# A hybrid encoder layer on one Trainium2 core: the second token group's projections, nine pairs of them as block products in a stage of their own, and attention as one stream over all heads

## The chip, the cores and the metric

The kernel runs on one core of one Trainium2 chip. TensorE (PE) multiplies matrices out of SBUF into PSUM, VectorE (DVE), ScalarE (ACT) and GpSimd (POOL) work element by element, and SyncE (SP) issues most of the transfers between DRAM and SBUF. The metric is the device time of one execution in microseconds; less is better.

## What the reference computes

One layer over 1280 tokens (a prompt of 1024 and a sample of 256), with 2048 channels, in fp32:

```
h    = rmsnorm(x, norm_w)
proj = h @ w_in                    # 2048 -> 4*1024 + 5*1024 + 16 columns
na_q, na_k, na_v, na_g, ml_qk, ml_v, ml_o, ml_z, ml_gp = split(proj)
att  = neighbourhood_attention(na_q, na_k, na_v, rpb) * silu(na_g)      # 8 heads of 128, 8 x 16 window
qk   = silu(centred_depthwise_conv(ml_qk, width 5))                     # 2048 channels
h    = bidirectional_mlstm(*split(qk), ml_v, gates(ml_gp))              # 4 heads of 256
mem  = rmsnorm(h) * sigmoid(ml_o) * silu(ml_z)
y    = rmsnorm(x + concat(att, mem) @ w_out, final_norm_w)
```

Prompt and sample go through the same weights; attention, convolution and mLSTM don't cross from one to the other.

## The kernel before, in words

Each fp32 operand of a large matmul is split into a high part (a cast by ACT, L156) and a low part (the difference, by DVE, L157), and each product takes three matmuls: high by high, high by low, low by high. So a product over 128 input channels is three passes, and a projection over 2048 channels is 48.

The tokens are worked on in two groups. Group A is tokens 0 to 767, group B the last 256 of the prompt and the 256 of the sample, 512 in all. Output channels come in blocks of 128, numbered: 0 to 7 are Q of the attention heads (`QT0`), 8 to 15 K (`KT0`), 16 to 23 the gate G (`GT0`), 24 to 39 the convolved channels of the mLSTM (`QK0`; 24 to 31 its Q, 32 to 39 its K), 40 to 47 O (`OT0`), 48 to 55 Z (`ZT0`). Two neighbouring blocks form a *pair*, named by its first number. V is projected in eight *units* V0 to V7 (`proj_v`), V4 with the 16 mLSTM gate columns beside it.

The program has three parts.

1. *Group A.* Each pair is computed in `pair_a` by seven block products in place of eight: tokens, input channels and output channels are halved, and sums of blocks are multiplied. For a pair's weights, POOL forms four sums of blocks in `summed` (L499), named by their product's number: 5, 6, 7 and 3. They live in SBUF only.
2. *Group B.* `proj_pair` computes a pair as 96 matmuls of 128x512 (L641): four loads of 512 KB of weights (`w_piece`, L618), eight splits of 512 columns, and a scaling by the inverse norm (L242). Q and K are stored split, convolved channels go through the convolution (L398, L404, L410), the rest is stored as it is to the scratch `pT` in DRAM. `proj_v` has 192 matmuls of 256 columns (272 in V4; L728). Group B's input is split when it is first used (`LazyX`, L149).
   Attention runs among these projections. After the projections of two attention heads and one mLSTM head, `run` emits their units at high priority: neighbourhood attention (`na_sample`, `na_prompt`) and mLSTM (`ml_units`). Blocks G, O and Z of group B come last, in `late_gate`: attention has by then stored its result without that factor for the tokens of group B, and `late_gate` reads it back from the scratch `mixT` (`lt`, L693), multiplies and stores it again (L695).
3. *W_out.* `product` (L1462, 128x512) multiplies the mixed channels, again by seven block products. `mix_block` loads the 32 blocks of `mixT` (L1342), `y_init` the residual (L1419), both issued by SP.

The order on each engine comes from the scheduler of the tile framework, which simulates the program and takes instructions by priority, and from the buffers of each pool: PSUM has three banks tagged "pr" and five tagged "a"; `po` is a ring of 520-column buffers; the pool "att" holds attention's buffers and is opened before the first pair of group B.

Of the kernel before, what the change touches and what calls it, by code (L numbers as in the profile page):

```python
# [35 lines left out]
XFIRST = (0, 1, 8, 9, 2, 3, 10, 11, 4, 5)  # L36
QT0, KT0, GT0, QK0, OT0, ZT0 = 0, 8, 16, 24, 40, 48


@with_exitstack  # L40
def kernel(
# [41 lines left out]
    qb = [dram.tile([P, 4], F32, tag=f"qb{n}", name=f"qb{n}") for n in range(16)]  # L83

    ident = const.tile([P, P], F32, tag="ident", name="ident")
    make_identity(nc, ident)
# [368 lines left out]
    def pair_a(n1, bg=iter(()), hook=None):  # L455
# [31 lines left out]
        for r in range(4):  # L487
# [122 lines left out]
    def po(name):  # L610
        return wb.tile([P, 520], F32, tag="po", name=name, bufs=NPO)
# [9 lines left out]
    def w_split(raw, lo_, hi_, name):  # L621
# [3 lines left out]
        return t  # L625

    FORTH = ((0, 1), (0, 0), (1, 0))

    def proj_pair(n1, X, late=False):
# [16 lines left out]
        for j in range(2):  # L646
            o = po(f"pco{n1}_{j}")
            if QK0 <= n1 < OT0:
# [8 lines left out]
                )  # L657
                cv = po(f"pcv{n1}_{j}")
                for _ in conv_taps(cv, o, ct, 516, 0):
                    pass  # L660
                hi = wb.tile([P, 520], F32R, tag="po", name=f"pch{ct}", bufs=NPO)
                store_conv(ct, cv, hi, o, ((0, 258, GA - 2), (260, 516, TP)))
                continue
# [12 lines left out]

    def late_gate(n1, k0, X):
        os_ = None
        if k0 >= 8:
            os_ = proj_pair(n1, X, True)  # L680
            for o_ in os_:
                S.activation(o_, o_, AF.Tanh, scale=0.5)
            n1 += ZT0 - OT0
        for j, z_ in enumerate(proj_pair(n1, X, True)):
            k = k0 + j
# [3 lines left out]
            sc = 0.5  # L689
            if k >= 8:  # L690
                V.scalar_tensor_tensor(z_, os_[j], 1.0, z_, op0=ALU.add, op1=ALU.mult)
                sc = w4_sb[:, k - 8 : k - 7]
            DM.dma_start(th, mixT[k][:, GA:])  # L693
            V.scalar_tensor_tensor(z_, th, sc, z_, op0=ALU.mult, op1=ALU.mult)
            DM.dma_start(mixT[k][:, GA:], z_)  # L695

    def proj_v(u, X):
# [38 lines left out]
        for tt in range(nt):  # L736
# [3 lines left out]
            if gates:  # L740
# [3 lines left out]
                )  # L744

    att_ctx = ExitStack()
    ap = att_ctx.enter_context(tc.tile_pool(name="att", bufs=2))

# [37 lines left out]
    def na_sample(h):  # L786
# [35 lines left out]
        o = na_tile("nst", [P, NAK], f"{nm}ot", 3)[:, :TS]  # L822
        S.copy(o, b[:, :TS])
        DM.dma_start(mixT[h][:, TP:], o)
        yield

    def na_prompt(h):
# [3 lines left out]
        def setup():  # L831
# [4 lines left out]
            o = na_tile("not", [P, TP], f"{nm}o", 1)  # L836
            DM.dma_start(o[:, :GA], pT[GT0 + h][:, :GA])
            hd["q"], hd["k"], hd["o"] = q, k, o
            yield

        def block(c4):
# [48 lines left out]
            for o, m in ends:  # L890
# [8 lines left out]
            cs = slice(c4 * 16, c4 * 16 + 16)  # L899
            ng = GA // 64  # L900
            V.scalar_tensor_tensor(
                ov[:, :ng, cs], bv[:, :ng], 0.5, ov[:, :ng, cs], op0=ALU.mult, op1=ALU.mult
            )
            S.copy(ov[:, ng:, cs], bv[:, ng:])
            if c4 == 3:
# [7 lines left out]
    def ml_tris():  # L913
        t = mid("tris")
        return [
# [4 lines left out]
    def ml_gates(sq, tris):  # L920
# [6 lines left out]
        def sm(name):  # L927
            return ap.tile([P, nt, 8], F32, tag=f"{nm}{name}", name=f"{nm}{name}", bufs=1)

        bd, bo, em = (sm(n) for n in ("bd", "bo", "em"))  # L930
        tmp = mid(f"{nm}tmp")
        lf, e, PL, EX, tot, mc, a1, mF = (
# [22 lines left out]
        rows = []  # L955
        rfi, rma = ([f(hf(f"{nm}r{w_}{i}"))[0:8, :TP] for i in range(2)] for w_ in "im")
        for r_, (w_, src) in enumerate((("f", lf), ("i", ig))):
# [42 lines left out]
        ei, w = (sm(n) for n in ("ei", "w"))  # L1000
        so = ap.tile([P, nt // 2, 8], F32, tag=f"{nm}so", name=f"{nm}so", bufs=1)
        b = bank("a", f"{nm}mp")
        mc2 = mc.rearrange("p t c -> p (t c)")
        for i, (base, cm, dst) in enumerate(((1 - P, 1, mL), (0, -1, mF))):
            sel = mid(f"{nm}sel{i}", P)
            G.memset(sel, 1.0)
# [38 lines left out]
    def ml_units(sq, h, gates):  # L1045
# [98 lines left out]
        def out_unit(J):  # L1144
# [114 lines left out]
            for et in range(2):  # L1259
                ch = 2 * h + et  # L1260
                na = min(max(GA - c0, 0), 256)
                z_ = sml(f"{n2}zr{et}")
# [42 lines left out]
    X = LazyX()  # L1305
    rbs[1] = late.tile([P, GB], F32, tag="rstdb1", name="rstdb1")
    for i in range(ML_H):
        proj_v(4 + i, X)
        if i == 0:
            x_stats(1, lambda c: mid(f"xdg1_{c}", 256))  # L1310
        for n in (QK0 + 8 + 2 * i, QK0 + 2 * i):
            proj_pair(n, X)
        if i == 0:
            with tc.high_priority():
                tris = ml_tris()
                gates = {sq: ml_gates(sq, tris) for sq in ("p", "s")}
        proj_v(i, X)
        for n in (QT0 + 2 * i, KT0 + 2 * i):
            proj_pair(n, X)
        run(  # L1320
            [u for sq in ("s", "p") for u in ml_units(sq, i, gates[sq])],
            [u for h in (2 * i, 2 * i + 1) for u in (na_sample(h), *na_prompt(h))],
        )
    for ch in range(0, 8, 2):
        late_gate(OT0 + ch, 8 + ch, X)

    for h in range(0, NA_H, 2):
        late_gate(GT0 + h, h, X)
    att_ctx.close()
# [84 lines left out]
    def y_init(p, q):  # L1414
        th, nh = divmod(q, 2)
        for tt in range(NT):
            y_ = Y[p, q, tt] = xslot(q * NT + tt, f"y{p}_{q}_{tt}")
            r0 = (th * NT + tt) * P
            DM.dma_start(y_, xtok[r0 : r0 + P, (2 * p + nh) * 512 : (2 * p + nh + 1) * 512])  # L1419

# [208 lines left out]
```

## Time and profile before

| what | value |
| --- | --- |
| runs of the kernel | 2581.06, 2582.97, 2585.05 us; median 2582.97 us |
| profiled execution | 2580.7 us, span 2579.0 us, granted clock 0.999 |
| TensorE busy | 2556.8 us, 99% |
| VectorE, ScalarE, GpSimd busy | 1899.7 us (74%), 1285.1 us (50%), 578.3 us (22%) |
| transfers | 465.67 MB, 181 GB/s on average |

In the profile's time line, group A ends at about 1097 us, V4 begins there, attention's units run from some 1190 to 2038 us, the last late gates end at 2181 us, and W_out takes the rest. A row of busy time names the line of the code, the engine, the operation and the tiles (output, then inputs). Matmuls are pipelined, so the time of one is best taken from many in a row.

### The profile page before, as it was taken

The page shows a single profiled execution, that of the slowest core. Times are in us where ns is not written, and L with a number is a line of the kernel's source. Part 1 is how long each engine was busy: PE and PEld are TensorE (multiplying, and loading weights), DVE is VectorE, ACT ScalarE, POOL GpSimd, SP SyncE. Part 2 cuts the span into 40 slices and gives each one's busy share as a digit, 9 for nine tenths or more (in the row PEclk, how much of TensorE's full clock was granted, in tenths as well). Part 3 has the DMA queues.
Part 4 walks back from the last instruction along what each step waited for, and adds up shares of the span by engine and source line. Part 5 has one row for each costly group of instructions (what it writes and reads, how often), then busy time and mean ns, then how long its engine had stood idle before and what let it go on. Part 6 is the DMA issues. An engine that isn't in the chain of part 4 may idle for free.

```text
span 2579.0 us, 42461 instructions
## 1 busy us (share of the span) xinstructions
PE 2556.8 (99%) x14406; PEld 2353.4 (91%) x14406; DVE 1899.7 (74%) x3878; ACT 1285.1 (50%) x2959; POOL 578.3 (22%) x857
## 2 busy tenths in 40 slices
PE   8999999999999999999999999999999999999998
PEld 8999999999999999988989989989888888888886
DVE  8768878887879798875477577567567544879695
ACT  8534545444444444544466466556466432345445
POOL 0435555444444444310000001000001000000001
PEclk9999999999999999999999999999999999999999
DMA  6534443434333343546787778777776567646327
GB/s 213 174 115 147 135 151 119 123 111 123 123 105 131 101 145 99 166 144 223 228 264 253 242 233 284 245 238 260 220 253 214 160 241 256 214 126 207 96 86 253
DMA packets 269505, 465.67 MB, mean 181 GB/s; under 512 B 45760, under 2 KB 154984, under 8 KB 269288
## 3 DMA queue, kind: packets, MB, share of 16 engines
q1 hardware_dynamic: 269288, 462.95, 55.9%
q8 instruction: 114, 1.87, 0.3%
q14 instruction: 103, 0.84, 0.1%
HBM read 354.78 MB, written 108.08 MB: 179 GB/s over the span
## 4 chain that ended last, share of the span: by engine, by line
PE 82%; DMA 3%; DVE 1%; issue 1%; SPq 0%; ACT 0%; ACTq 0%; POOLq 0%; POOL 0%; DVEq 0%
PE pc L641 22%; PE po L1462 15%; PE pv L728 6%; PE A16b L265 1%; PE A48b L265 1%; PE A40b L265 1%; PE A52b L265 1%; PE A20b L265 1%; PE A44b L265 1%; PE A54b L265 1%; PE A46b L265 1%; PE A22b L265 1%; PE A14b L265 1%; PE A70b L265 1%; PE A38b L265 1%; PE A50b L265 1%
## 5 line engine op out<-in xcount | busy, mean ns | idle before, releaser
L1462 PE MATMUL po<-wo,mo 128*128 128x512 f32 x1620 | 375.3, 393 | 0.0
L1462 PEld LDWEIGHTS po<-wo,mo 128*128 128x128 f32 x1620 | 303.9, 188 | 70.6 <-DVE y L1412 0.3
L157 DVE TENSOR_TENSOR ws<-wr,ws 128x512 fp32r<-128x512 f32 x224 | 152.5, 690 | 126.7 <-ACT ws L156 125.7
L156 ACT CAST ws<-wr 128x512 fp32r<-128x512 f32 x224 | 137.0, 619 | 200.0 <-PE pc L641 136.2
L107 POOL TENSOR_SCALAR rs<-rs 128x1 f32<-128x1 f32 x10 | 3.4, 341 | 552.5 <-DVE rs L1442 552.4
L156 ACT CAST mo<-mb 128x640 fp32r<-128x640 f32 x72 | 51.6, 726 | 106.0 <-PE po L1462 92.1
L157 DVE TENSOR_TENSOR mo<-mb,mo 128x640 fp32r<-128x640 f32 x72 | 58.5, 820 | 33.9 <-ACT mo L156 33.9
L1412 DVE TENSOR_TENSOR y<-y,po 128x512 f32<-128x512 f32 x90 | 58.3, 682 | 10.7 <-PE po L1462 10.5
L404 DVE SCALAR_TENSOR_TENSOR pcv<-pco,cw_sb,pcv 128x516 f32<-128x516 f32 x64 | 48.4, 757 | 21.9 <-ACT pcv L398 21.2
L157 DVE TENSOR_TENSOR wsv<-wr_v,wsv 128x512 fp32r<-128x512 f32 x64 | 44.0, 692 | 21.7 <-ACT wsv L156 21.4
L156 ACT CAST mo<-ms 128x640 fp32r<-128x640 f32 x40 | 29.0, 727 | 60.8 <-PE po L1462 33.6
L156 ACT CAST wsv<-wr_v 128x512 fp32r<-128x512 f32 x64 | 39.1, 616 | 40.1 <-PE pc L641 21.5
L242 DVE TENSOR_TENSOR pco<-pc,rstdb 128x512 f32<-128x512 f32 x48 | 33.1, 689 | 29.1 <-PE pc L641 28.5
L107 POOL TENSOR_SCALAR mls_0r<-mls_0r 128x2 f32<-128x2 f32 x4 | 1.2, 300 | 196.8 <-ACT mls_0jk L1248 196.8
L1425 ACT ACTIVATE jk<-y 128x512 f32<-128x512 f32 x40 | 25.2, 631 | 35.3 <-DVE y L1412 35.1
L157 DVE TENSOR_TENSOR mo<-ms,mo 128x640 fp32r<-128x640 f32 x40 | 32.7, 820 | 7.3 <-ACT mo L156 7.3
L120 ACT ACTIVATE xq<-xq 128x1024 f32<-128x1024 f32 x20 | 21.2, 1061 | 31.1 <-DMA xq<-in_xtok_dram 30.6
L641 PE MATMUL pc<-x_0h,ws 128*128 128x512 f32 x112 | 36.0, 398 | 0.0
L641 PE MATMUL pc<-x_1h,ws 128*128 128x512 f32 x112 | 35.3, 397 | 0.0
L641 PE MATMUL pc<-x_9h,ws 128*128 128x512 f32 x112 | 34.7, 398 | 0.0
L641 PE MATMUL pc<-x_8h,ws 128*128 128x512 f32 x112 | 34.6, 395 | 0.0
L265 PE MATMUL fb<-xg,fw 128*128 128x384 f32 x192 | 34.6, 334 | 0.0
(1628 smaller groups left out, 8144.1 us busy)
## 6 DMA issues: line engine op xcount, KB each, us to landing
wr<-in_w_in_dram SPq DMA_DIRECT2D x112, 512.0 KB, 4.1
wr_v<-in_w_in_dram SPq DMA_DIRECT2D x32, 512.0 KB, 4.0
wb<-in_w_o_dram SPq DMA_DIRECT2D x48, 256.0 KB, 3.6
xq<-in_xtok_dram SPq DMA_DIRECT2D x20, 512.0 KB, 4.5
mb<-mx SPq DMA_DIRECT2D x32, 320.0 KB, 6.4
y<-in_xtok_dram SPq DMA_DIRECT2D x40, 256.0 KB, 4.0
wr_wp<-in_w_o_dram SPq DMA_DIRECT2D x16, 512.0 KB, 4.4
vS<-vo SPq DMA_DIRECT2D x24, 256.0 KB, 4.1
```

Of the source, the lines that this page charges most:

```text
L107: G.tensor_scalar(out, ssum, 1.0 / count, EPS, op0=ALU.mult, op1=ALU.add)
L120: S.activation(raw, raw, AF.Square, accum_out=ssq[g][:, t, q : q + 1])
L156: S.copy(hi, src)
L157: V.tensor_tensor(lo, src, f(hi), op=ALU.subtract)
L242: V.tensor_tensor(o, src, rb, op=ALU.mult)
L265: PE.matmul(o, w(a_), x(b_), start=first and m == 0, stop=last and m == 2)
L404: V.scalar_tensor_tensor(dst[:, a:n], src[:, a + j - pad : n + j - pad], cw_sb[:, ct, j : j + 1], dst[:, a:n], op0=ALU.mult, op1=ALU.add,)
L641: PE.matmul(pb[j], t[j][:, wi, c : c + P], xs[xi], start=first and m == 0, stop=last and m == 2,)
L728: PE.matmul(outs[tt], xs[:, tt * P : (tt + 1) * P], t[:, wi, q * w : (q + 1) * w], start=first and m == 0 and (gates or tt % 2 == 0), stop ...
L1412: V.tensor_tensor(Y[p, q, tt], Y[p, q, tt], bk, op=op)
L1425: S.activation(jk, Y[p, q, tt], AF.Square, accum_out=ss[t][:, c : c + 1])
L1462: PE.matmul(bk[tt], m[xi][:, tt * P : (tt + 1) * P], w[wi], start=first and kk == 0 and j == 0, stop=last and j == 2, skip_group_check=True,)
```

## The change

Nine pairs of group B (16, 32, 18, 24, 8, 20, 10, 22 and 12) leave `proj_pair` and are computed by the new `pair_s` as seven block products of 128x256, with 168 matmuls in place of 96 of twice the width. Each takes three blocks of the weights from `w_in` and four sums of blocks from the new scratch `sD`, which `pair_a` fills while it handles the same pair for group A. `operand_sums` forms the sums of group B's input blocks once. The products are folded into four quarters by ACT and DVE, and `finish_s` scales, convolves or gates and stores them while the next pair runs.

The order of group B becomes: V4, the gates, V0, pair 0 (`QT0`), `operand_sums`, the nine pairs; then the pool of that stage is closed, and "att" is opened on its memory; then the other pairs and V units as fill for attention, which is one `run` over all heads, with the mLSTM units spread evenly among the attention units (`paced`); then `late_gate` for O and Z alone. G of group B is ready before attention now, so attention multiplies by it over all tokens. Last, `mix_block` and the first half of `y_init` are issued by POOL in place of SP, and `mix_block`'s groups change order.

```diff
@@ pair_a
+                if n1 in SECOND and i in SUMS:
+                    DM.dma_start(sD[n1, i][:, r * 256 : (r + 1) * 256], src[i])
@@ na_sample
-        S.copy(o, b[:, :TS])
+        DM.dma_start(o, pT[GT0 + h][:, TP:])
+        V.scalar_tensor_tensor(o, b[:, :TS], 0.5, o, op0=ALU.mult, op1=ALU.mult)
@@ after the pools of group B
+    def operand_sums():
+        for kk in range(8):
+            raw = xs2.tile([P, 2, 512], F32, tag="raw2", name=f"xq2_{kk}", bufs=3)
+            for h in range(2):
+                DM.dma_start(raw[:, h], xT[:, kk + 8 * h, GA:])
+                S.mul(raw[:, h], raw[:, h], lnw_sb[:, kk + 8 * h : kk + 8 * h + 1])
+            a, b, c, d = (raw[:, h, t * 256 : (t + 1) * 256] for h in range(2) for t in range(2))
+            V.tensor_tensor(d, d, b, op=ALU.subtract)
+            V.tensor_tensor(b, b, a, op=ALU.subtract)
+            V.tensor_tensor(a, d, a, op=ALU.add)
+            V.tensor_tensor(c, c, a, op=ALU.subtract)
+            for h in range(2):
+                t = xs2.tile([P, 2, 512], F32R, tag=f"s{h}{kk}", name=f"xs{h}_{kk}")
+                split(t[:, 0], t[:, 1], raw[:, h])
+                sums[h, kk] = t
+    def pair_s(n1, tag, bg):
...
+        for s_, (i, bk, first) in enumerate(steps):
+            pool, tag_, n = ((xs2, "raw2", 3), (wb, "wraw", 2))[s_ % 2]
+            raw = pool.tile([P, 1024], F32, tag=tag_, name=f"{nm}r{i}", bufs=n)
+            if i in BLOCK:
+                DM.dma_start(raw.rearrange("p (r c) -> p r c", r=4), w_in[n1 // 2]...)
+            else:
+                DM.dma_start(raw, sD[n1, i])
+            for q in range(2):
+                t = pool.tile([P, 2, 544], F32R, tag="wsp", name=f"{nm}s{i}{q}", bufs=(4, 3)[q])
+                split(t[:, 0, :512], t[:, 1, :512], raw[:, q * 512 : (q + 1) * 512])
+                for k in range(4):
...
+                    for m, (wi, xi) in enumerate(FORTH):
+                        PE.matmul(bk, t[:, wi, k * P : (k + 1) * P], xs[xi], ...)
+            with tc.high_priority():
+                if i == 1:
+                    S.copy(c0, x0)
+                elif i == 2:
+                    V.tensor_tensor(c0, c0, y0, op=ALU.add)
...
+            if s_ % 2:
+                next(bg, None)
...
+        return finish_s(n1, Cn)
@@ the order of group B
+    proj_v(4, X)
+    x_stats(1, lambda c: po(f"xdg1_{c}")[:, :256])
+    with tc.high_priority():
+        tris = ml_tris()
+        gates = {sq: ml_gates(sq, tris) for sq in ("p", "s")}
+    proj_v(0, X)
+    proj_pair(QT0, X)
+    operand_sums()
+    bg = iter(())
+    for i, n in enumerate(SECOND):
+        bg = pair_s(n, ("pr", "a")[i % 2], bg)
...
+    s_ctx.close()
+    ap = att_ctx.enter_context(tc.tile_pool(name="att", bufs=2))
     for i in range(ML_H):
...
+            elif u not in SECOND and u != QT0:
+                proj_pair(u, X)
...
+    run(
+        [
+            u for i in range(ML_H)
+            for u in paced((u for sq in ("s", "p") for u in ml_units(sq, i, gates[sq])), len(na[i]))
+        ],
+        [u for us in na for u in us],
+    )
+    for ch in LATE:
+        late_gate(ch, X)
-    for h in range(0, NA_H, 2):
-        late_gate(GT0 + h, h, X)
@@ W_out
-        DM.dma_start(t, mixT[8 * kh + kk][:, th * TH : (th + 1) * TH])
+        G.dma_start(t, mixT[8 * kh + kk][:, th * TH : (th + 1) * TH])
     Ad = [mix_block(1, 0, kk) for kk in range(8)]
+    Ae = [mix_block(0, 1, kk) for kk in range(8)]
+    Ac = [mix_block(1, 1, kk) for kk in range(8)]
     Aa = [mix_block(0, 0, kk) for kk in range(8)]
-    Ac = [mix_block(1, 1, kk) for kk in range(8)]
-    Ae = [mix_block(0, 1, kk) for kk in range(8)]
...
-            DM.dma_start(y_, xtok[...])
+            q_ = DM if p else G
+            q_.dma_start(y_, xtok[...])
```

Three places show how the order moves. On TensorE, before, the end of pair 0 (`pc0`) is followed by pair 8 (`pc8`); `x1_` are the input's high and low parts, `ws_` the weights'.

```order
L641 MATMUL pc0_1_13799<-x1_15h_12931,ws_0_31_13901 128x512 x2
L641 MATMUL pc0_1_13799<-x1_15l_12932,ws_0_31_13901 128x512
L641 MATMUL pc8_0_13952<-x1_0l_12624,ws_8_00_13956 128x512
L641 MATMUL pc8_0_13952<-x1_0h_12623,ws_8_00_13956 128x512 x2
L641 MATMUL pc8_0_13952<-x1_1l_12633,ws_8_00_13956 128x512
```

At the same place after, pair 16 begins in `pair_s`, with the first 256 tokens of group B:

```order
L658 MATMUL pc0_1_13635<-x1_15h_13111,ws_0_31_13737 128x512 x2
L658 MATMUL pc0_1_13635<-x1_15l_13112,ws_0_31_13737 128x512
L1375 MATMUL S16bx_13908<-x1_0l_12804,S16s10_13915 128x256
L1375 MATMUL S16bx_13908<-x1_0h_12803,S16s10_13915 128x256 x2
L1375 MATMUL S16bx_13908<-x1_1l_12813,S16s10_13915 128x256
```

Both fences show matmuls in threes; the width halves, and the pair's output takes the place of the next pair's.

On VectorE, before, V0's first split (`wsv_0_0_0`) stands between the splits and convolutions of pairs 24 and 32 and the gates' arrays (`mg`):

```order
L157 TENSOR_TENSOR ws_24_30_13262<-wr_24_3_13260,ws_24_30_13262 128x512
L979 COPY mgstmp_13506<-mgsmc_13537 128x2x4
L157 TENSOR_TENSOR ws_24_31_13265<-wr_24_3_13260,ws_24_31_13265 128x512
L404 SCALAR_TENSOR_TENSOR pcv32_1_13145<-pco32_1_13140,cw_sb_921,pcv32_1_13145 128x516 x4
L979 COPY mgstmp_13506<-mgsmc_13537 128x2x4
L157 TENSOR_TENSOR wsv_0_0_0_13558<-wr_v0_0_13556,wsv_0_0_0_13558 128x512
L984 TENSOR_TENSOR mgstmp_13506<-mgstmp_13506 128x16
```

After, it stands among the operand sums (`xq2`) and their splits (`xs0`, `xs1`):

```order
L1327 TENSOR_TENSOR xq2_1_13803<-xq2_1_13803 128x256
L1325 TENSOR_TENSOR xq2_2_13818<-xq2_2_13818 128x256
L166 TENSOR_TENSOR xs0_0_13797<-xq2_0_13788,xs0_0_13797 128x512
L1328 TENSOR_TENSOR xq2_1_13803<-xq2_1_13803 128x256
L1326 TENSOR_TENSOR xq2_2_13818<-xq2_2_13818 128x256
L166 TENSOR_TENSOR xs1_0_13800<-xq2_0_13788,xs1_0_13800 128x512
L166 TENSOR_TENSOR xs0_1_13812<-xq2_1_13803,xs0_1_13812 128x512
L166 TENSOR_TENSOR wsv_0_0_0_13394<-wr_v0_0_13392,wsv_0_0_0_13394 128x512
```

The pairs' work has gone from before V0, and the operand sums have come in.

POOL issued no transfer before. After, at the start of W_out, its queue ends with the residual's loads (`y0`), the last two blocks of `mixT` (`mb116`, `mb117`) and the final norm:

```order
L1566 DMA y0_2_3_27177<-in_xtok_dram 128x512
L1566 DMA y0_2_4_27179<-in_xtok_dram 128x512
L1566 DMA y0_3_0_26700<-in_xtok_dram 128x512
L1488 DMA mb116_26456<-mx14_149 128x640
L1488 DMA mb117_26458<-mx15_150 128x640
L116 TENSOR_SCALAR rs5_29151<-rs5_29151 128x1
L117 TENSOR_TENSOR rs5_29151<-rs5_29151,mhalf_220 128x1
```

Before, the same two blocks stood on SP among the last late gates' reads, stores and weights:

```order
L693 DMA lt15_24585<-mx15_150 128x512
L695 DMA mx14_149<-pco54_0_24574 128x512
L695 DMA mx15_150<-pco54_1_24576 128x512
L1342 DMA mb116_25234<-mx14_149 128x640
L618 DMA wr_18_0_24740<-in_w_in_dram 128x1024
L1342 DMA mb117_25236<-mx15_150 128x640
```

So the blocks no longer share SP's queue with the weights, and on POOL they stand behind the 20 loads of the residual.

More of the change, by code (lines that the diff above doesn't have):

```diff
@@ L83 @@
     qb = [dram.tile([P, 4], F32, tag=f"qb{n}", name=f"qb{n}") for n in range(16)]
+    sD = {
+        (n, i): dram.tile([P, 1024], F32, tag=f"sD{n}_{i}", name=f"sD{n}_{i}")
+        for n in SECOND for i in SUMS
+    }
     ident = const.tile([P, P], F32, tag="ident", name="ident")
@@ L625, in w_split, with conv_b @@
         return t
+    def conv_b(o, ct):
+        cv = po(f"pcv{ct}")
+        yield from conv_taps(cv, o, ct, 516, 0)
+        hi = wb.tile([P, 520], F32R, tag="po", name=f"pch{ct}", bufs=NPO)
+        store_conv(ct, cv, hi, o, ((0, 258, GA - 2), (260, 516, TP)))
     FORTH = ((0, 1), (0, 0), (1, 0))
@@ new lines, in finish_s @@
+    def finish_s(n1, Cn):
+        for j, o in enumerate(Cn):
+            if QK0 <= n1 < OT0:
+                ct = n1 - QK0 + j
+                DM.dma_start(o[:, 0:4], qb[ct])
+                for z in (260, 518):
+                    G.memset(o[:, z : z + 2], 0.0)
+                yield from conv_b(o, ct)
+                continue
+            o = o[:, :GB]
+            if n1 < GT0:
+                store_qk(
+                    n1 + j, o,
+                    lambda dt: wb.tile([P, 520], dt, tag="po", name=f"S{n1}_{j}_{dt}", bufs=NPO),
+                    PARTS_B,
+                )
+                yield
+                continue
+            if OT0 <= n1 < ZT0:
+                S.activation(o, o, AF.Tanh, scale=0.5)
+            elif n1 >= GT0:
+                th = po(f"S{n1}th{j}")[:, :GB]
+                S.activation(th, o, AF.Tanh, scale=0.5)
+                V.scalar_tensor_tensor(o, th, 1.0, o, op0=ALU.add, op1=ALU.mult)
+            DM.dma_start(pT[n1 + j][:, GA:], o)
+            yield
```

146 lines of the change are left out of this document (96 added, 50 removed).

## The prediction

> **What bounds the kernel now.** I read the page first, then the stages as windows, then the chain that ended last.
>
> ```profile
> span 2579.0 us, 42461 instructions
> ...
> PE 2556.8 (99%) x14406; PEld 2353.4 (91%) x14406; DVE 1899.7 (74%) x3878; ACT 1285.1 (50%) x2959; POOL 578.3 (22%) x857
> ...
> PE 82%; DMA 3%; DVE 1%; issue 1%; SPq 0%; ACT 0%; ACTq 0%; POOLq 0%; POOL 0%; DVEq 0%
> ```
>
> TensorE is busy 99% of the span and carries 82% of the chain. All other engines together hold it up for about 22 us (2579.0 less 2556.8), so a gain can only come from fewer matmul columns, and a loss only from waits that aren't there yet. The windows are cut at the stages: group A, the boundary, attention among group B's projections, the late gates, W_out.
>
> ```profile
> core 0: us, PE busy (x) PEld busy (x) DVE busy (x) ACT busy (x) POOL busy (x), PEclk, DMA share, GB/s
> 0.00:1097.00 1097.00, 1086.61 (x6269) 1081.31 (x6270) 906.34 (x1656) 546.69 (x1296) 494.33 (x560) 1.00 0.43 135
> 1097.00:1190.00 93.00, 93.00 (x592) 82.31 (x591) 69.35 (x189) 40.08 (x73) 9.34 (x41) 1.00 0.52 164
> 1190.00:2030.00 840.00, 837.10 (x5206) 751.37 (x5205) 540.64 (x1442) 480.72 (x1197) 62.51 (x236) 1.00 0.75 241
> 2030.00:2181.00 151.00, 151.00 (x662) 122.80 (x661) 67.13 (x105) 42.80 (x75) 0.00 (x0) 1.00 0.64 219
> 2181.00:2579.00 398.00, 389.14 (x1685) 315.64 (x1683) 316.23 (x490) 174.84 (x320) 12.10 (x20) 0.99 0.52 170
> ```
>
> The granted clock is full everywhere (1.00). In the three middle stages, all that the change rebuilds, TensorE idles 2.9 us in 1084. The few waits that it has there are of this kind:
>
> ```profile
> PE nas_0t L781 <- ACT mlp_1x L1213: 1.0, 1, 1.0
> PE nap_0s L764 <- DVE mlp_2zr L1269: 1.0, 1, 1.0
> ```
>
> What a matmul costs is best read from runs of one line in the chain of waits (start, duration, count):
>
> ```profile
> 2053.93 128.03 PE pc L641 x551
> 1244.40 10.48 PE pv L728 x89
> 1097.71 14.98 PE pv L728 x120
> ```
>
> 128.03/551 is 232.4 ns for 128x512, 10.48/89 is 117.8 ns for 128x256. The third row is unit V4, whose matmuls have 272 columns: 124.8 ns. So time goes by columns, with no charge for the shorter form.
>
> **The change, part by part.**
>
> *The nine pairs.* Each loses 96 matmuls of 512 and gets 7 products x 8 row pieces x 3 passes = 168 of 256: 19.79 us for 22.31. Over nine pairs: 864 x 0.2324 = 200.8 us go, 1512 x 0.1178 = 178.1 us come, **−22.7 us** on the path. The far bound takes 124.8 ns for each: −12.1 us. I take the 117.8, since 272 columns explain the other row. The number of attention and W_out matmuls stays.
>
> *Feeding them.* A pair's splits grow from 8 to 14 of 512 columns, and nine folds of 256 are new.
>
> ```profile
> L157 DVE TENSOR_TENSOR ws<-wr,ws 128x512 fp32r<-128x512 f32 x224 | 152.5, 690 | 126.7 <-ACT ws L156 125.7
> L156 ACT CAST ws<-wr 128x512 fp32r<-128x512 f32 x224 | 137.0, 619 | 200.0 <-PE pc L641 136.2
> L164 DVE TENSOR_TENSOR fw<-fr,fw 128x256 fp32r<-128x256 f32 x32 | 12.7, 420 | 2.0 <-ACT fw L163 2.0
> ...
> 1300.00:1400.00 100.00, 100.00 (x674) 92.30 (x673) 80.07 (x222) 64.27 (x163) 8.88 (x33) 1.00 0.84 266
> ```
>
> DVE per pair: 14 x 0.690 + 5 x 0.420 + 2 x 0.690 = 13.1 us, 66% of 19.8. ACT: 14 x 0.619 and four copies, some 10 us, 53%. Loads: 7 x 512 KB = 3.67 MB in 19.8 us, 185 GB/s. The last row is a stretch of before in which DVE was 80% busy, ACT 64%, and DMA moved 266 GB/s, while TensorE didn't idle. Inside the stage: 0.
>
> *The boundary.* Between V4's first matmul and S16's last, DVE must now do the operand sums as well as the gates. By the changed order it has 249 instructions there: 55 splits (x 0.690 = 38.0), 16 low parts of the input, 32 adds of 256 (x 0.420 = 13.4), and 146 others, most of them small arrays of the gates.
>
> ```profile
> 1087.50 1.29 DVE L157 TENSOR_TENSOR wsv<-wr_v,wsv 128x512 fp32r<-128x512 f32 x2 [1.31 <-ACT wsv L156]
> 1107.06 0.75 DVE L149 SCALAR_TENSOR_TENSOR x_12l<-xr,lnw_sb,x_12h 128x512 fp32r<-128x512 f32 x1
> 1107.72 0.75 DVE L149 SCALAR_TENSOR_TENSOR x_13l<-xr,lnw_sb,x_13h 128x512 fp32r<-128x512 f32 x1
> L1018 DVE TENSOR_TENSOR mgpw<-mgpw,mgptmp 128x4 f32<-128x4 f32 x24 | 2.8, 144 | 0.0
> ...
> DVE ws L157 <- ACT ws L156: 5.8, 4, 2.2
> DVE mgptmp L979 <- PE mgpmc L976: 3.1, 2, 2.0
> ```
>
> The low parts are 16 x 0.75 = 12.0. The others lie between 146 x 0.119 = 17 (the gate row, 2.8/24) and 146 x 0.367 = 54 (the mean of the boundary window, 69.35/189); my sum by kinds is 45.7. Together 109 us of durations, between 81 and 117. Two such rows stand 0.66 us apart for 0.75 us each (1107.06 and 1107.72), so packed rows take 0.88 of their sum: 96 us, between 71 and 103. TensorE's work over the same stretch is 192 x 0.1248 + 192 x 0.1178 + 96 x 0.2324 + 168 x 0.1178 = 88.7, with the gates' own small matmuls 96. DVE starts 10.2 us ahead (1087.50 against 1097.71). So DVE may idle 10 us before TensorE waits. In the boundary window of before it idled 93 − 69.35 = 23.7 us, part of it for ACT and TensorE (last two rows). The stall lies between 0 and 14; I take **+3 us**, near the low end, since most of the idling in before is DVE being done early.
>
> *Attention's late start.* Its pool now takes the memory that the stage frees, so its loads wait on SP for S12's last reader, and V5's and pair 34's weights queue behind them. To the first prompt tile some 9.2 MB go out in that order.
>
> ```profile
> 1200.00:1210.00 10.00, 9.96 (x49) 8.08 (x48) 4.08 (x11) 3.36 (x9) 0.00 (x0) 1.00 0.93 322
> ```
>
> At 322 GB/s that is 28.5 us, at the 266 of the row above 34.5. TensorE has V5 (192 x 0.1178 = 22.6 us) and half a pair (11.2 us) until then: 33.8 us, but pair 34's weights are due at 28. Stall between 0 and 6: **+1.5 us**.
>
> *Attention as one stream.* Lines L641 and L728 fill that stretch of before:
>
> ```profile
> 1190.00:2030.00 840.00, 466.94 (x1853) 338.34 (x1854) 1.00 0.75 241
> 1190.00:2030.00 840.00, 159.19 (x1221) 150.43 (x1219) 1.00 0.75 241
> ```
>
> By counts the fill is 1853 x 0.2324 + 1221 x 0.1178 = 574.5 us, which leaves attention 262.6 us of TensorE, 31%. After, the fill is 6 V units (135.7), 10 pairs (223.1) and 8 late pairs (178.5) less 46.5 that stand behind the last attention matmul: 490.8. Attention becomes 35% of 753 us. DVE goes from 64% to about 68%, DMA stays near 260 GB/s. Waits here are 1 us each now; I take 0, between −3 and +6. The late read and write of four gate pairs goes, but it lay under the window 2030 to 2181, where TensorE idles nothing: 0.
>
> *The block sums' stores.* 144 issues of 128 KB are new on SP, in front of weight loads of group A.
>
> ```profile
> 535.92 0.33 SPq L494 DMA_DIRECT2D A62r<-in_w_in_dram  x1
> ...
> 561.03 7.36 SPq L494 DMA_DIRECT2D A20r<-in_w_in_dram  x2
> ```
>
> An issue takes about 0.33 us, 48 us over 1000; SP waits up to 7.36 us at a time for buffers there, and the DMA share is 0.43. They hide in that: 0, at most 2 us.
>
> *W_out's loads from POOL.* 32 block loads and 20 of the residual change from SP to POOL, in order.
>
> ```profile
> L108 POOL TENSOR_TENSOR rs<-rs,mhalf 128x1 f32<-128x1 f32 x10 | 8.7, 869 | 0.8
> L499 POOL TENSOR_TENSOR A14t<-A14r 128x256 f32<-128x256 f32 x8 | 11.6, 1444 | 8.7 <-DVE A14s L164 5.3 <-DVE A12s L164 3.4
> mb<-mx SPq DMA_DIRECT2D x32, 320.0 KB, 6.4
> L157 DVE TENSOR_TENSOR mo<-mb,mo 128x640 fp32r<-128x640 f32 x72 | 58.5, 820 | 33.9 <-ACT mo L156 33.9
> ```
>
> The first can go some 40 us before W_out starts (6 us behind attention). The last two blocks stand behind the residual loads; they are needed 48.8 us after that start (a product of 120 matmuls at 0.2324, then six steps of 15), less 6.4 us to land and some 4 us to split (0.82 a split, ACT's copy before it, some slack): issued by +38.6. That allows 78.6/52 = 1.51 us per issue; each 0.1 us above costs 5.2 us. No row shows a POOL-issued load. Nearest are an SP issue (0.33) and POOL's own rows (0.87 for a tiny one, 1.44 for 256 columns), all below 1.51: 0.
>
> Sum: −22.7 + 3 + 1.5 = **−18.2 us**. The profiled execution took 2580.7 us (1.7 beyond its span), 2.3 below the median of 2582.97. 2582.97 − 18.2 is **2565 us**.
>
> **The rivals.**
>
> *POOL's issues are too slow* (slower). Place: the start of W_out, at block loads 31 and 32. It decides from 1.51 us an issue. [...] For it: POOL's 1.44-us row, and 20 loads queued ahead in order. Against: POOL's row with next to no data takes 0.87, and an issue moves no data through POOL itself.
> [...] No run here shows a POOL-issued load beside VectorE. I give the lock 0.05 of this rival's chance.
>
> *Both new boundaries stall at their far ends.* DVE at the operand sums (14) and the loads at attention's start (6): −22.7 + 20 = −3, 2580 us, no change. For it: the whole stage waits behind one event, twice. Against: the 10-us lead.
>
> *Attention can't follow the faster pace* (slower). Its chains between ACT, DVE and TensorE ran over 840 us and get 753. Each per cent short costs 7.5 us; 5% gives 2565 + 37.5 = 2602 us. For it: all units are issued ahead of the fill, and a late unit blocks TensorE's queue in order. Against: waits of 1 us in the window now, and 31 to 35% is little.
>
> The counts of matmuls in the changed order exclude that the change doesn't do what it says.
>
> **How the numbers follow.** Forecast 0.60, POOL 0.14 (the lock in it), boundaries 0.13, attention's pace 0.13. A measurement can tell 0.2%, 5.2 us, from no change. The forecast lies below 2577.8 with its bounds (−22.7 + 20 is the second rival's). The POOL rival is slower in 0.12 and within in 0.02, the boundaries' split 0.05 faster, 0.05 same, 0.03 slower; attention's is slower in 0.10 and within in 0.03. Faster 0.65, same 0.10, slower 0.25. Low end: −22.7 with nothing lost and 3 us won in attention, 2557, rounded down to 2556. High end: 2590, the POOL rival at 2.0 us, which leaves out most of the third rival and the tail of the first.
>
> **What would show it.** Right: runs of the S blocks' line at 118 ns a matmul; TensorE idle under 5 us between V4 and pair 34; POOL's issue rows near 1 us, with blocks 31 and 32 landed before W_out's third product; waits of TensorE in attention still 1 us each. Wrong: an S matmul over 124 ns, TensorE waiting for DVE's splits of xs, TensorE waiting in W_out for the last blocks, or attention's last matmul nearer to W_out than 40 us because units come late.

## The result and the profile after

The changed kernel ran in 2567.36, 2565.82, 2563.00 and 2563.56 us, median 2564.69; the kernel before, beside it, in a median of 2583.06. The ratio is 0.993, with a 95% interval of 0.9913 to 0.9947: 18.4 us faster. Run once more unaltered among the last experiments it came to 2566.04 against 2581.84, ratio 0.9941 (0.9929 to 0.9953), 15.8 us. The forecast was 2565. That the total fits hides that the parts do not, which is what the rest is about.

The profiled execution is the slowest of the first four, 2567.36 us. Its page:

```profile
span 2565.5 us, 44500 instructions
...
PE 2534.0 (99%) x15054; PEld 2367.4 (92%) x15054; DVE 1968.9 (77%) x4029; ACT 1336.5 (52%) x3041; POOL 610.6 (24%) x909
...
q0 software_dynamic: 4160, 15.73, 1.6%
...
PE 77%; DMA 3%; DVE 2%; ACT 0%; issue 0%; SPq 0%; POOL 0%; ACTq 0%; POOLq 0%; DVEq 0%
```

TensorE is still the bound, 22.8 us less busy. The queue q0 is new: the loads issued by POOL. The windows, cut at V4's first matmul, at S16's (the first of the nine pairs), at S12's end and at W_out's start (columns as before):

```profile
0.00:1103.85 1103.85, 1088.71 (x6273) 1082.66 (x6273) 906.46 (x1656) 544.92 (x1297) 493.74 (x560) 1.00 0.47 151
1103.85:1180.14 76.29, 75.64 (x539) 70.08 (x539) 68.55 (x196) 47.67 (x87) 7.82 (x19) 1.00 0.64 217
1180.14:1356.55 176.41, 176.41 (x1533) 175.99 (x1532) 138.52 (x255) 104.70 (x201) 0.40 (x6) 1.00 0.69 224
1356.55:2162.50 805.95, 802.19 (x5035) 722.62 (x5034) 539.35 (x1435) 464.21 (x1141) 87.75 (x289) 1.00 0.78 262
2162.50:2565.50 403.00, 391.02 (x1681) 316.05 (x1679) 315.99 (x490) 174.99 (x319) 20.88 (x36) 0.99 0.51 172
```

Before, V4 began at 1097.55 and W_out at 2181.80 us:

```profile
0.00:1097.55 1097.55, 1087.16 (x6272) 1081.86 (x6273) 906.89 (x1657) 547.24 (x1297) 494.33 (x560) 1.00 0.43 135
1097.55:2181.80 1084.25, 1081.35 (x6456) 956.55 (x6455) 677.38 (x1734) 563.04 (x1343) 71.84 (x277) 1.00 0.72 231
2181.80:2579.00 397.20, 388.34 (x1681) 315.01 (x1679) 315.43 (x489) 174.84 (x320) 12.10 (x20) 0.99 0.52 169
```

So group A takes 6.3 us more (1103.85), group B 25.6 less (1058.65 for 1084.25), W_out 5.8 more (403.0 for 397.2): −13.5 in this execution.

The stage of nine pairs never leaves TensorE idle: 176.41 of 176.41 us busy. Of its 1533 matmuls, 1512 are the block products; the others are, but for one, the gates'. Two neighbouring pieces of its chain of waits show what a matmul costs:

```profile
1205.13 2.79 PE S32by L1375 x24
1207.91 2.72 PE S32bx L1375 x24
```

The first, product 2, reads the plain input: 116 ns. The second, product 6, reads the operand sums: 113.3 ns. Over all 1512, from start to start, the mean is 115.4 ns. TensorE's waits in group A and in attention:

```profile
PE A56v L459 <- DVE A56vo L166: 2.3, 2, 1.2
PE A58v L459 <- DVE A58vo L166: 2.1, 1, 2.1
PE nap_0s L769 <- DMA nap3qk<-kS: 1.9, 1, 1.9
PE A60v L459 <- DVE A60vo L166: 1.0, 1, 1.0
PE mls_0s L1091 <- DVE mls_0d L1190: 1.0, 1, 1.0
```

Those for A56v and A58v were 0.2 and 0.4 us before, and A60v had none; they are transposes of V's outputs in group A. The loss at W_out's start is best followed from the chain (first row), TensorE's timeline (second) and small windows:

```profile
2156.36 14.33 DMA wr_wp<-in_w_o_dram
...
2171.44 29.58 PE L1609 MATMUL po<-wo,mo 128*128 128x512 f32 x120 [1.84 <-ACT wo L165]
...
2169.00:2172.00 3.00, 1.16 (x5) 0.65 (x4) 1.41 (x2) 1.96 (x4) 1.51 (x3) 1.00 1.03 384
2172.00:2174.00 2.00, 2.00 (x7) 1.56 (x6) 1.92 (x4) 0.95 (x2) 1.17 (x3) 0.58 1.04 389
2174.00:2176.00 2.00, 2.00 (x7) 1.57 (x6) 0.00 (x0) 0.00 (x0) 0.98 (x3) 0.57 1.05 392
2176.00:2178.00 2.00, 2.00 (x11) 1.62 (x10) 0.47 (x1) 0.73 (x1) 0.74 (x2) 1.00 1.02 369
```

A piece of W_out's weights takes 14.33 us from issue to landing while the DMA engines are full (1.03 and more, 384 to 392 GB/s). TensorE waits 1.84 us for it, and then the granted clock is 0.58 and 0.57 for 4 us, which costs 4 x 0.425 = 1.7 us more.

### The profile page after: what moved, and what is told of

It is laid out like the page before. It is cut to its first block, busy times and chain, and to the rows that moved or that the text cites. A ratio compares the mean times of both kernels' runs of the same rounds, so it can differ in the third digit from the quotient of the medians.

```text
span 2565.5 us, 44500 instructions
## 1 busy us (share of the span) xinstructions
PE 2534.0 (99%) x15054; PEld 2367.4 (92%) x15054; DVE 1968.9 (77%) x4029; ACT 1336.5 (52%) x3041; POOL 610.6 (24%) x909
## 4 chain that ended last, share of the span: by engine, by line
PE 77%; DMA 3%; DVE 2%; ACT 0%; issue 0%; SPq 0%; POOL 0%; ACTq 0%; POOLq 0%; DVEq 0%
PE pc L658 16%; PE po L1609 15%; PE pv L736 5%; PE A52b L274 1%; PE A44b L274 1%; PE A40b L274 1%; PE A48b L274 1%; PE A20b L274 1%; PE A50b L274 1%; PE A42b L274 1%; PE A18b L274 1%; PE A54b L274 1%; PE A70b L274 1%; PE A68b L274 1%; PE A36b L274 1%; PE A46b L274 1%
## 5 line engine op out<-in xcount | busy, mean ns | idle before, releaser
L166 DVE TENSOR_TENSOR ws<-wr,ws 128x512 fp32r<-128x512 f32 x152 | 105.0, 700 | 50.8 <-ACT ws L165 50.1
L165 ACT CAST ws<-wr 128x512 fp32r<-128x512 f32 x152 | 92.5, 617 | 68.0 <-PE pc L658 56.0
L165 ACT CAST wsv<-wr_v 128x512 fp32r<-128x512 f32 x64 | 38.9, 616 | 22.7 <-PE pv L736 11.5
L413 DVE SCALAR_TENSOR_TENSOR pcv<-pco,cw_sb,pcv 128x516 f32<-128x516 f32 x48 | 36.3, 757 | 8.0 <-ACT pcv L407 7.9
L251 DVE TENSOR_TENSOR pco<-pc,rstdb 128x512 f32<-128x512 f32 x30 | 20.6, 686 | 18.0 <-PE pc L658 17.9
L274 PEld LDWEIGHTS fb<-xg,fw 128*128 128x128 f32 x192 | 33.4, 188 | 0.0
L1521 DVE TENSOR_TENSOR ms<-mb,mb 128x640 f32<-128x640 f32 x40 | 32.7, 818 | 0.0
L774 DVE CUSTOM_DVE_ANT_0 nap_0st<-nap_0s,nap_0bt 128x384 f32<-128x384 f32 x32 | 17.7, 554 | 19.2 <-PE nap_0s L769 8.7
L1488 POOL DMA_DIRECT2D mb<-mx x32 | 17.7, 556 | 59.1 <-DVE ws L166 24.7
```

The lines of the kernel that those rows point to most:

```text
L165: S.copy(hi, src)
L166: V.tensor_tensor(lo, src, f(hi), op=ALU.subtract)
L251: V.tensor_tensor(o, src, rb, op=ALU.mult)
L274: PE.matmul(o, w(a_), x(b_), start=first and m == 0, stop=last and m == 2)
L413: V.scalar_tensor_tensor(dst[:, a:n], src[:, a + j - pad : n + j - pad], cw_sb[:, ct, j : j + 1], dst[:, a:n], op0=ALU.mult, op1=ALU.add,)
L1521: V.tensor_tensor(t, x, y_, op=op)
```

## The experiments

Ratios are to the kernel before, on the same chip, with 95% intervals. The changed kernel stands at 0.993 and 0.9941. *Stalls* of a stretch are the sum of what TensorE's matmuls are spaced beyond the median of their kind.

**The nine pairs as plain pairs.** The stores of block sums in group A go, `proj_pair` gates the blocks of G before it stores them, as `finish_s` does, and `pair_s` and `operand_sums` give way to:

```diff
-    operand_sums()
-    bg = iter(())
-    for i, n in enumerate(SECOND):
-        bg = pair_s(n, ("pr", "a")[i % 2], bg)
+    for n in SECOND:
+        proj_pair(n, X)
```

> The nine pairs go back to 96 matmuls of 128x512 each, at the same place in the new order, with neither the operand sums nor the stores of block sums; attention as one stream, the gates and the loads from POOL stay. Theory (the gain is TensorE columns): the stage of nine pairs takes 9 x 22.3 = 200.8 us in place of the 176.4 of the changed kernel, group A loses the 6.3 us that the profile of the changed kernel shows there: 18 us slower than the changed kernel, about 2583 us. Rival (the new order of attention and gates brought the gain, the block products only pay for their own feeding): within 4 us of the changed kernel, 2561 to 2569 us.

Measured: 1.0008 (0.9999 to 1.0017), 2587.8 against 2585.93 us: no gain is left. Its three stages (columns as before):

```profile
0.00:1099.85 1099.85, 1089.35 (x6272) 1084.43 (x6273) 909.12 (x1656) 546.72 (x1296) 488.89 (x560) 1.00 0.43 134
1099.85:2181.19 1081.34, 1080.05 (x6456) 956.65 (x6456) 682.05 (x1733) 559.04 (x1305) 95.29 (x313) 1.00 0.70 230
2181.19:2587.40 406.21, 391.32 (x1681) 315.79 (x1679) 316.34 (x490) 174.92 (x319) 20.88 (x36) 0.99 0.52 171
```

V4 to W_out took 1081.3 us, 22.7 more than the changed kernel's 1058.65: TensorE is busy 25.8 us more there (1080.05 for 1054.24) and waits 3.1 less. Attention's first matmul came at 1295 us, within the nine pairs, so this undoes the wait for memory too. The gain is the block products'. The new order by itself shortens group B by 2.9 us against before and makes W_out 9.0 longer: it brings nothing over the old, and W_out's loss comes without the block products too.

**No stores of block sums.**

```diff
-                if n1 in SECOND and i in SUMS:
-                    DM.dma_start(sD[n1, i][:, r * 256 : (r + 1) * 256], src[i])
...
-                DM.dma_start(raw, sD[n1, i])
+                DM.dma_start(raw, w_in[n1 // 2, SUMS.index(i)])
```

> The 144 stores of block sums in group A are left out; the nine pairs read rows of the input weights of the same size in their place, so the output is not the reference's. Theory (the stores stand on SP between the loads and stores of group A, and hold up the buffers that V's group A waits for): V4 starts at 1097.6 us as before the change, not at 1103.9, the waits for A56vo, A58vo and A60vo are gone, 6 us faster than the changed kernel, about 2559 us. Rival (the late V4 is chance of that one execution, or the shorter transfers themselves share the DMA engines): V4 stays within 2 us of 1104, or group A is as long without the waits; 2564 us.

Measured: 0.9914 (0.99 to 0.9927). TensorE's waits from 150 to 520 us:

```profile
PE A58v L459 <- DVE A58vo L166: 0.9, 1, 0.9
PE A56v L459 <- DVE A56vo L166: 0.4, 1, 0.4
```

1.3 us of such waits against 5.4, and V4 began at 1100.57 us, 3.3 sooner. In seven profiles whose group A is that of the changed kernel, V4 began between 1102.2 and 1106.9 us. Part of the scatter is the clock: this execution had a stretch at half clock, which costs 1.7 us and which the changed kernel's group A did not have:

```profile
95.36:98.75 3.39, 3.39 (x9) 2.79 (x10) 3.39 (x6) 0.87 (x3) 2.52 (x4) 0.50 0.10 7
```

Without it V4 would have begun 5 us sooner than in the changed kernel. So the stores cost 3 to 5 us by V4's start, 4 to 7 by the ratios.

**Those stores from POOL, and from ACT.** First `G.dma_start` in place of `DM.dma_start`, then `S.dma_start` behind the cast of the same sum.

> The 144 stores of block sums are issued by POOL, which makes the sums, in place of SP. Theory (it is SP's order that costs, not the transfers): V4 at 1098 us, as without the stores, about 2559 us. Rival (the transfers themselves, or POOL's sums, which come 144 x 0.56 = 81 us of issue later in all): V4 at 1104 us or later, 2565 us or more.

> The 144 stores of block sums are issued by ACT, each behind the cast of the same sum, in place of SP. Theory (on SP they stand before V's stores of group A, on POOL before the next sums; ACT has time and has waited for the sum already): the stalls between 200 and 500 us, 7.5 us in the changed kernel and 11 with POOL, fall to the 2.7 of the kernel before; 2560 us. Rival (the transfers themselves delay V's stores): 7 us of stalls there as in the changed kernel, 2565 us.

Both missed: 0.9948 (0.9936 to 0.9961) and 0.9945 (0.9934 to 0.9957), V4 at 1109.24 and 1105.41 us. From ACT the wait for V's earlier store did shrink; the rows are ACT's waits from 200 to 500 us, of the changed kernel and then of this one:

```profile
ACT A56vo L165 <- DMA vS<-A56vo: 13.3, 5, 4.4
```

```profile
ACT A56vo L165 <- DMA vS<-A56vo: 4.2, 3, 1.9
```

But V4 came no earlier than with the stores on SP, and with POOL later than in any of those profiles. So SP's order is one way in which the stores cost, and the other queues have their own; which, these runs don't settle.

**Pair 14 for pair 12 among the nine.** `KT0 + 6` in place of `KT0 + 4` in `SECOND`.

> Pair 14 takes the place of pair 12 among the nine. In group A, pair 12 runs from 332 to 365 us beside the storing of V, pair 14 from 365 to 395 with little of it. Theory (the stores cost where they meet V's): the stall of 2.3 us at 355 us is gone, and 2 us are won. Rival (the stores cost wherever they stand): as many stalls between 200 and 500 us, within 1 us of the changed kernel.

Measured: 0.996 (0.9947 to 0.9974), not faster. In group A the stall at 356 us went as the theory said, from 2.4 us (control) to 0.55. V4 began at 1102.76 us, which lies within the scatter of 1102.2 to 1106.9. What the stall had cost was given back at W_out's start, where TensorE waited as follows (2090 to 2260 us, the control first):

```profile
PE po L1609 <- ACT wo L165: 2.8, 2, 1.9
PE po L1609 <- DVE wo L166: 0.8, 2, 0.5
```

```profile
PE po L1609 <- ACT wo L165: 5.1, 2, 3.8
PE po L1609 <- DVE wo L166: 1.7, 1, 1.7
```

Attention's last matmul stood 42.7 us before W_out here, 46.6 in the control.

**Block loads and residual on SP again.** `DM.dma_start` in `mix_block` and `y_init`.

> The 32 block loads of W_out and the 20 first residual loads go back to SP; all else as changed. Theory (an issue on POOL takes 0.556 us, far below the 1.51 us from which it decides, so the queue hardly matters): within 2 us of the changed kernel, 2563 to 2567 us. Rival (POOL-issued loads land later, 8.2 us against 6.4, and the 1.8-us wait and the 5.8 us by which W_out is longer come from them): W_out back to 397 to 398 us, about 2559 us. Rival on the other side (on SP the block loads stand in front of the last late gates' weights and hold TensorE up there): 2 to 6 us slower than the changed kernel.

Measured: 0.996 (0.9948 to 0.9973), 5 to 8 us slower than the changed kernel: the rival on the other side. SP's timeline near the end of group B:

```profile
2139.46 0.33 SPq L629 DMA_DIRECT2D wr<-in_w_in_dram  x1
2140.24 7.40 SPq L1488 DMA_DIRECT2D mb<-mx  x9
2148.20 0.33 SPq L629 DMA_DIRECT2D wr<-in_w_in_dram  x1
...
2153.17 7.13 SPq L1566 DMA_DIRECT2D y<-in_xtok_dram  x8
2160.54 0.33 SPq L629 DMA_DIRECT2D wr<-in_w_in_dram  x1
```

The last pair's pieces (`wr`) stand behind nine block loads and behind eight residual loads, and TensorE waits 2.64 and 3.61 us for them; over the 4 us after each wait the granted clock was 0.64 and 0.57:

```profile
2155.97 0.50 PE L658 MATMUL pc<-x_4l,ws 128*128 128x512 f32 x1 [2.64 <-ACT ws L165]
2167.22 0.69 PE L658 MATMUL pc<-x_6l,ws 128*128 128x512 f32 x1 [3.61 <-ACT ws L165]
```

W_out itself took 399.6 us, 3.4 less than in the changed kernel, so the loads from POOL do cost there; on SP they cost more ahead of it. Before the change the same loads on SP did no harm. Attention's last matmul then came 128.1 us before W_out (2053.7, later than the 2038 given above, to 2181.8), and now 46.6 (2115.9 to 2162.5). That this shorter distance is the reason fits these runs; none changes it alone.

**Only the residual on SP.** `q_ = DM` in `y_init`.

> Only the 20 residual loads go back to SP, the 32 block loads stay on POOL. With both on SP the last late pair waited 6.6 us for its weights. Theory A (the residual loads do it: they wait on SP for input buffers that only the last late pair frees, and its last weight piece stands behind the first of them): the same waits in the last late pair, 8 to 11 us slower than the changed kernel. Theory B (the 32 block loads do it, by standing in front of the weights): no wait there, within 3 us of the changed kernel or faster, since the residual no longer delays the last blocks.

Measured: 0.9952 (0.994 to 0.9965), 3 us over the control's median, with overlapping intervals. The last pair no longer waits, against theory A. TensorE stands 4.4 us between that pair and W_out, whose first weights now stand behind nine residual loads on SP, and 1.9 us in W_out's first product, as in the control. So the last pair's waits came with the block loads, and the residual costs less and elsewhere.

**Block loads in halves.**

```diff
-        G.dma_start(t, mixT[8 * kh + kk][:, th * TH : (th + 1) * TH])
+        for z in range(2):
+            lo = th * TH + z * TH // 2
+            G.dma_start(t[:, z * TH // 2 : (z + 1) * TH // 2], mixT[8 * kh + kk][:, lo : lo + TH // 2])
```

> Each of the 32 block loads is issued as two halves of 320 columns, so POOL issues 84 loads in place of 52. The trace of the changed kernel shows an issue of 0.55 us and the next one 1.1 us behind it. Theory (the price of the first rival: time is free up to 78.6 us from the first issue to the last, and counts in full beyond): 84 x 1.1 = 92 us, 14 us slower, with TensorE waiting in W_out for the last blocks. Rival (the 1.1 us is the transfers' own pace, half a block takes half of it): 64 x 0.6 + 20 x 1.1 = 60 us, no slower than the changed kernel within 3 us.

Measured: 0.9962 (0.995 to 0.9975), 5.4 us over the control, between the two. The 84 loads spread over 83 us (2117.6 to 2200.6), of which POOL stood 9.6 waiting for the last gates' stores. The first 60 half blocks went out 0.84 us apart on average, where 30 whole blocks in the changed kernel came 1.16 apart, so a half takes neither the whole time nor half of it. TensorE waited twice for VectorE's splits of the blocks (first row); ahead of the first of these waits VectorE had waited for what the last late gates read back (second row):

```profile
PE po L1611 <- DVE mo L166: 5.1, 2, 2.8
...
2178.99 0.75 DVE L702 SCALAR_TENSOR_TENSOR pco<-lt,w_sb,pco 128x512 f32<-128x512 f32 x1 [7.93 <-DMA lt<-mx]
```

The last half blocks left 28 us after W_out's start, still inside the 38.6 that the prediction allowed. So the theory's path, the last blocks coming late, isn't what the trace shows.

**Attention in four runs again.** The one `run` over all heads becomes one for each pair of heads, emitted behind its projections.

> Attention goes back to one run for each pair of attention heads and mLSTM head, emitted after the projections that it needs, as before the change; the stage of nine pairs and all else stay. Theory (the gain is columns; one stream over all heads only spreads attention's waits, of which there are 4 us): within 3 us of the changed kernel, 2563 to 2569 us, with attention's last matmul nearer to W_out or as near. Rival (without the stream attention would run out of work between heads, or end so late that its stores come after the late gates): 8 us or more slower than the changed kernel, over 2572 us.

Measured: 0.9979 (0.9969 to 0.9988), 10 to 13 us slower than the changed kernel. Attention ended 36.7 us before W_out, 10 us closer, and TensorE then waited in W_out, with the clock at 0.50 for 6.8 us after each of the two longest waits:

```profile
PE po L1605 <- ACT wo L165: 9.0, 3, 4.5
PE po L1605 <- DVE wo L166: 1.1, 1, 1.1
```

The forecast had called the stream worth nothing. By this run it is worth what it keeps free behind attention.

**No operand sums.** The call of `operand_sums` goes, and the four products read `X`.

> The operand sums (16 loads, 32 additions and 16 splits) are left out; the four products that used them take group B's plain input, so the output is not the reference's; matmuls, splits of weights and folds stay as many. Theory (the sums hide in DVE's 10-us lead at the boundary): within 2 us of the changed kernel, V4's start to S16's end at most 2 us shorter. Rival (they cost what the far bound said): S16 begins 6 to 14 us earlier after V4. A second question: a matmul of 256 columns took 113.3 ns in the products on the sums and some 118 in those on the plain input; if the place of the operand does it, the nine pairs' stage gets 4 x 24 x 9 x 0.0045 = 3.9 us longer (180 us), if the product does it, it stays at 176.4.

Measured: 0.996 (0.9948 to 0.9972), not faster but 5 to 8 us slower. The trace has 1.6 us of that in the nine pairs and 2 in W_out; the rest is open. V4 to S16 took 77.7 us (1104.81 to 1182.52) against 76.3 with the sums, of which TensorE waited 0.65, so they hide almost wholly. The nine pairs' stage took 178.0 us for 176.4, which seems to lie between the two answers. But with the sums the stage also held some 20 matmuls of the gates, 2 us of them, which came before it here. The block products alone (line L1375; TensorE busy, weight loads, clock, DMA) are clearer, with the sums first:

```profile
1180.14:1356.55 176.41, 174.90 (x1512) 174.13 (x1511) 1.00 0.69 224
```

```profile
1182.52:1360.55 178.03, 178.03 (x1512) 177.85 (x1511) 1.00 0.70 220
```

They take 3.1 us more, where 3.9 was expected if the operand decides and none if the product does. From start to start the mean on the sums was 113.8 ns and on the plain input 117.1; with every product on the plain input it is 117.7. So it is the operand that is read, and not the product.

**Twelve pairs.** `SECOND` gets 34, 14 and 26 as well.

> Pairs 34, 14 and 26 join the nine, so twelve pairs are block products and attention keeps 6 V units and 15 pairs as fill. Theory (a pair of block products is worth 22.3 − 19.3 = 3 us, and attention follows): 9 us less 1 to 3 us for 48 more stores, 2557 to 2559 us. Rival (attention, with 38% of its stretch, can't follow the pace, at 7 us a per cent): no gain, 2565 us or more, with TensorE waiting in attention.

Measured: 1.0027 (1.0018 to 1.0037), slower than before the change. TensorE waited only some 6 us within attention, but attention used up the fill behind it: three pairs (67 us) had gone from its fill, and it became only 25 us shorter (724 for 749), so all late gates were drawn in between its units. Its last matmul (2161.9 us) was followed by W_out itself. The blocks' buffers lie in the memory that attention frees, and their loads from POOL came only then (TensorE's wait, POOL's first block loads, two windows):

```profile
PE po L1610 <- DMA wb<-in_w_o_dram: 26.8, 1, 26.8
...
2176.47 3.76 POOL L1489 DMA_DIRECT2D mb<-mx  x7 [16.87 <-DMA wb<-in_w_o_dram]
...
2162.00:2188.00 26.00, 0.00 (x0) 0.00 (x0) 9.44 (x16) 4.93 (x8) 6.21 (x12) 0.57 1.01 382
2188.00:2192.00 4.00, 3.29 (x8) 2.64 (x9) 2.61 (x4) 0.00 (x0) 1.83 (x4) 0.50 1.02 388
```

**The changed kernel as control.**

> The changed kernel once more, unaltered, as the measure for the runs beside it. 18 us faster than before by its first runs (ratio 0.993); stalls of 7 to 10 us between 200 and 500 us, a wait near 2 us in W_out's first product.

As expected: 0.9941, a wait of 1.9 us in W_out's first product, stalls of 9.5 us between 200 and 500. Its W_out took 403.0 us, as in the first profile, its group A 3 us more.

## Why the prediction was right, and where it was not

*Columns, −22.7.* Right, and some 3 us low. The block products were busy 174.9 us, so the term is 200.8 − 174.9 = −25.9 us. It took the V units' 117.8 ns for every matmul; those on the operand sums take 113.8 on average. The run with plain pairs confirms the size (25.8 us of TensorE's busy time).

*The boundary, +3, and attention's start, +1.5.* The middle stages idle 0.65 + 3.76 = 4.4 us (windows) against 2.9 before: +1.5 for both terms and for attention's pace together. At the boundary TensorE waited 0.65 us: DVE's lead carried it. At attention's start the first prompt tile wasn't waited for; 1.9 us came later, at head 3's operands (`nap3qk`, 1641.7 us). Group B is then −25.9 + 1.5 = −24.4 for the measured −25.6. The 1.2 us left are busy time, and the run with plain pairs has as much without the block products (1080.05 for 1081.35), so they go with the new order.

*The stores of block sums, 0 and at most 2.* This step failed. I counted SP's time for 144 issues against its idle time; V's stores stand behind them in order, and ACT needs their buffers (from 200 to 500 us it waited 38.8 us for V's stores, 27.2 before). V4 came 6.3 us later, of which the run without stores gives back 3.3, or 5 without its stretch at half clock.

*W_out's loads from POOL, 0.* The price lay within the bounds, 0.55 us an issue and some 1.1 from one to the next for 1.51 allowed, and so did the place of the last two blocks. POOL's timeline has the last residual load, then those blocks:

```profile
2176.75 0.56 POOL L1566 DMA_DIRECT2D y<-in_xtok_dram  x1 [0.56 <-PE po L1609]
2190.63 0.55 POOL L1488 DMA_DIRECT2D mb<-mx  x1 [13.32 <-DMA mx<-pco]
2194.77 0.55 POOL L1488 DMA_DIRECT2D mb<-mx  x1 [3.59 <-DMA mx<-pco]
```

They left 28 and 32 us after W_out's start, inside the 38.6 that I allowed, held by the last gates' stores and not by the queue. The rival of slow issues did not come about: an issue took 0.55 us for 320 and 256 KB, and for 160 KB in the run with halves. Nor was one held up beside VectorE: the 35 that overlap an instruction of VectorE took 0.55 us, but for one of 0.76, and the 17 that overlap none took 0.55 or 0.56. So no run shows the 2.0 us an issue behind the high end of the range, nor a lock, which had 0.05 of this rival's chance. But the step asked only for the queue's time, not what its transfers take from others: 50 of the 52 loads fall in the 42 us before W_out and its first 15, and a piece of W_out's own weights takes 14.33 us to land. W_out is 5.8 us longer, 4.9 of it in its first 240 matmuls (31.41 + 28.96 us where before had 27.74 + 27.73). With the 52 loads on SP these took 28.07 + 27.71 us. So the loads' place does it; that they slow the weights by sharing the DMA engines fits the full engines in the windows (a share of 1.02 to 1.05), and no run separates it.

*The third rival* did not come about with nine pairs: waits of TensorE in attention were 3.8 us in all. With twelve attention did fall behind, and this showed in the distance from its end to W_out, not in waits inside it. The prediction had worked that distance out as 46.5 us (46.6 measured) and used it only for POOL's loads. The runs read as if it were the margin of the whole end: W_out took 403 to 406 us at 46.6, 407.5 at 42.7 (pair 14) and 415.3 at 36.7 (attention in four runs), for 397.2 at 128.1 before; with none left TensorE waited 27.

The sum of the profiled execution is +6.3 − 25.6 + 5.8 = −13.5, against −18.2; its other runs were 1.5 to 4.4 us faster, and the profiled one of before was 2.4 us faster than its median. So the mechanism, fewer columns, was right, and that the total came within 1 us was luck: group B gave 7 us more than its terms, and the two ends, both put at nothing, took about as much, or more.

## What to carry to other kernels

When fill is cut away beside a long side stream, work out where that stream now ends: the loads of the next stage must fit between its end and that stage. Here the loads on SP did no harm with 128.1 us of room; at 46.6 TensorE waited 2.64 and 3.61 us for weights that stood behind them, and with the loads on POOL W_out took 5.8 us more. A transfer added "in idle time" is priced by who stands behind it in its queue, as those weights did, and not by its issue alone (0.55 us on POOL); what lands beside it may count too, which no run here separates. A total that fits says little; compare stage by stage, and look whether a gain at one stage is given back at the next tight place, as with pair 14.

## What the hardware showed that I had not expected

A wait of TensorE cost twice in some places. After the 1.84-us wait at 2169.6 us the granted clock was 0.58 and 0.57 for 4 us; cut at its edges, the stretch is 3.4 us at half clock:

```profile
2172.33:2175.73 3.40, 3.40 (x10) 2.62 (x9) 1.59 (x3) 0.62 (x2) 1.74 (x4) 0.50 1.04 388
```

After the 26.8 us with twelve pairs the clock was 0.50 over the next 4 us. It wasn't so after every wait. In W_out's first product, waits of 1.80, 1.84, 1.87 and 1.91 us (the block sums' stores from ACT, the changed kernel, the residual on SP, no such stores) were followed by half clock, and waits of 1.68, 1.74 and 1.86 us (those stores from POOL, no operand sums, the control) were not. In group A, 2.22 us in the control was, and 2.75 us with the residual on SP was not. Every wait of 3.6 us or more after the first 100 us was. The stretches that go with these waits lasted 3.41, 6.83 or, with twelve pairs, 27.31 us, so 1, 2 or 8 times the shortest; the last lay mostly within the wait (0.57 in the window from 2162 to 2188 us). So 1.80 us of waiting was enough once and 2.75 us wasn't another time; what decides it was not found.

And matmuls of one shape cost 113.3 to some 122 ns by which operand they read. The run without the sums shows that the operand decides. Even tiles of the plain input differ: in the nine pairs those on `x_15h` came 113.3 ns apart on average, those on `x_9h` 121.9. What sets the tiles apart was not found.
